# Turning the last channel-major products of a hybrid decoder layer into token-major ones

## The chip, the cores and the metric

One core of a Trainium2 chip runs the whole layer in one program. The time is the device time of one execution in microseconds, and the figure for a kernel is the median of its runs. Everything is float32 in and out.

## The reference

One layer for 256 tokens (T) with 2048 channels (D), and 256 memory tokens. A normalised x, `h`, goes through one wide product, whose columns are cut among three branches; each branch goes back to D through a product of its own, is scaled by a sigmoid gate, and the sum goes through an output product and a last norm.

```python
h = rms_norm(x, norm_w)
(sb_q, sb_k, sb_v, sb_z, ssd_z, ssd_xbc, ssd_dt, mem_q, mem_z, gate_pre) = split(h @ w_in)
o_sb  = stick_breaking_attention(sb_q, sb_k, sb_v) * silu(sb_z)           # 8 heads of 128
xbc   = silu(causal_depthwise_conv(ssd_xbc, conv_w, conv_b))              # 4 taps, 4096 channels
x_ssm, b_in, c_in = split(xbc)                                            # 2048, 1024, 1024
y     = ssd_chunked_scan(x_ssm, dt, a, b_in, c_in) + d_skip * x_ssm
o_ssd = gated_group_rms_norm(y, ssd_z, ssd_norm_w)                        # 8 groups of 256
o_mem = memory_cross_attention(mem_q, mem_n, w_mem_kv) * silu(mem_z)      # 4 heads of 256
g_sb, g_ssd, g_mem = split(sigmoid(gate_pre + b_gate))
merged = g_sb*(o_sb @ w_branch_sb) + g_ssd*(o_ssd @ w_branch_ssd) + g_mem*(o_mem @ w_branch_mem)
return rms_norm(x + merged @ w_out, final_norm_w)
```

## The kernel before

Nearly all of the time goes into products of 256 tokens with weights that stream in from DRAM, 0.5 MB at a time. Such a piece is a **chunk**. Its load `raw` goes out on SP's queue (`load_chunk`, L205; four buffers). The products are taken in halves: each value is split in two (`split`, L142): ACT copies it into the high half `wh` (L146, type fp32r), DVE subtracts that from the value for the low half `wl` (L150); three buffers of each. A product of float32 is then three products of halves: high by high, high by low, low by high.

There are two ways to take a product.

- **Token-major** (`gemm`, L249): the activations are stationary, 512 columns of the weights move. A chunk is 2 k-tiles of 128 rows by 512 columns. For each k-tile and each half of the tokens there are three matmuls of 512 columns (L266, L267, L268): 12 for a chunk. Out come rows of tokens, 512 channels wide. The accumulator is evacuated 3 chunks after the product's end (LATE).
- **Channel-major** (`gemm_cols`, L211): the weights are stationary, 128 by 128. What moves are the activations: both halves side by side, 512 wide, past `wh` (L229), and the high half alone, 256 wide, past `wl` (L233). A chunk is 4 k-tiles by 256 columns, so 16 matmuls. Out come channels on partitions, tokens along the row, in two accumulators that `fold` (L239) adds: an ACT copy (L246) and a DVE add (L247), 2 chunks after the end (LATE_C).

Steps that need channels on partitions are the attention heads (q and k), the convolution, whose taps run along the tokens, and the gates z. The z products are token-major already and are **turned** by `to_turned` (L298): DVE transposes blocks of 32 by 32 out of the accumulator (L307, twice), ACT's queue sends them to a scratch in DRAM (L309, twice), and four DMAs from ACT's queue bring them back with the blocks in order (L316). The result has its tokens in a permuted order; the views `turned` and `blocked` (L321, L326) read it.

Each engine runs its instructions in the order in which the program emits them. Beside the chunks, two mechanisms set that order. `defer(fn, n)` puts a step into a heap, to be emitted n chunks later. `pump` (L185), called after each chunk, emits what is due and then moves one of two lanes on by a step; the lanes hold the attention heads and the 8 SSD groups as generators. A step that comes to ACT or DVE stands between the splits of two chunks, and the splits behind it wait for it.

The order of the products, with their chunks: memory values (16), kT (16, channel-major), qM (16, channel-major), zM and zS (32, turned), qS and kS (32, channel-major), vS (16), zT (32, turned), the convolution's xBC (64, channel-major), then for each branch four pairs of a gate product (8 chunks) and a branch product (4, 4 or 8 chunks), then the output product. The memory heads run beside qS to zT, the stick-breaking heads beside zT and the convolution, the SSD groups beside the first and the second branch.

In the convolution, `conv_evac` (L708) folds 256 channels into a tile `cu` and defers the four taps of each 128 channels (L717, L720: one DVE instruction of 256 tokens and three of 255, 254, 253), so that the last are emitted 5 chunks after the product's end. A list `waiting` (L725) holds the 12 tiles that get a silu: four of z, then B, C, and the four of x. Three are emitted for each of the last four groups of 512 channels, the last three of x 1, 2 and 6 chunks behind the convolution's end. They share a table with the copies; ACT loads another for the exponentials (L741) and for the sigmoids (L745).

A gate product's evacuation (L880) adds the bias on DVE and defers `sigmoid` (L744) by one chunk; the branch product's evacuation (L889) multiplies with it. Inside `ssd_group` (L750), ACT copies `cbs` (L775), takes exponentials of `dec` (L785), DVE weighs them (L789), and the sums y are added into the x tiles of cT (L812, L815).

## Time and profile before

| what | before |
|---|---|
| median of 3 runs | 1226.38 us (1225.35 to 1226.67) |
| profiled execution | 1225.48 us, span of the trace 1223.7 us |
| granted clock of TensorE | 0.998 of full speed |
| TensorE matmuls (PE) | 1213.0 us busy, 99% |
| weight loads of TensorE (PEld) | 1024.1 us, 84% |
| VectorE (DVE) | 781.5 us, 64% |
| ScalarE (ACT) | 640.7 us, 52% |
| GpSimd (POOL) | 50.4 us, 4% |
| DMA | 251.07 MB, 205 GB/s on average |
| chain of waits that ended last | PE 96%, DMA 1%, ACT 1%, DVE 1%, issue 1% |
| largest group on DVE | L150, 409 x 1232 ns |
| largest group on ACT | L146, 409 x 1056 ns |

The profile is of one execution, and times in it count from the start of its span. "Busy" counts instructions from start to end; matmuls overlap one another, so their lengths add up to more than the time that they take, and the distance of their starts is the better measure. In a row of the timeline stand the start, the length (of several, where the row ends in x2), the engine, the line, the operation, the tiles written and read, and in brackets how long the engine was idle just before, and who ended that wait. A row of groups has the count, the busy time and the mean of one in ns behind the bar. A table load of ACT (ACT_TABLE_LOAD) takes 1283 ns.

### The profile page before, as it was taken

Reading aid. Unit: us, or ns where it says so; the run is one execution under the profiler, and the core shown is the slowest. Engines: PE = TensorE matmul, PEld = TensorE weight load, DVE = VectorE, ACT = ScalarE, POOL = GpSimd, SP = SyncE. Lnnn points to the kernel's source line nnn. Section 1 sums busy time; section 2 is a strip of 40 time slices with the busy share of each in tenths; the row PEclk is TensorE's granted clock in tenths of the full one; section 3 lists DMA queues with packets and bytes.
Section 4 is the critical chain, followed back from the end, with each engine's and each line's share of the span. In section 5 each row is a group of like instructions: output and inputs, shape, how many; then the busy total and the mean of one; then the engine's idle time right before and its main releaser. Section 6 shows DMA issues by size and latency. Waiting matters only on the chain.

```text
span 1223.7 us, 16119 instructions
## 1 busy us (share of the span) xinstructions
PE 1213.0 (99%) x6132; PEld 1024.1 (84%) x6132; DVE 781.5 (64%) x990; ACT 640.7 (52%) x859; POOL 50.4 (4%) x50
## 2 busy tenths in 40 slices
PE   9999999999999999999999999999999999999997
PEld 7888888888888888888888888888888888888886
DVE  5686564556654555888887758676677755555554
ACT  6764533364444444545665757475756544444443
POOL 0000000000000000010100000000000010110101
PEclk9999999999999999999999999999999999999999
DMA  9966578875466778655668667576856666567673
GB/s 308 364 201 191 156 233 230 244 204 155 149 179 189 223 217 232 183 176 177 177 184 221 208 198 222 180 232 180 233 182 189 204 194 210 185 196 243 201 245 112
DMA packets 169646, 251.07 MB, mean 205 GB/s; under 512 B 11040, under 2 KB 85984, under 8 KB 169440
## 3 DMA queue, kind: packets, MB, share of 16 engines
q1 hardware_dynamic: 151840, 229.51, 61.7%
q10 hardware_dynamic: 17728, 20.53, 5.6%
q8 instruction: 48, 0.79, 0.3%
q14 instruction: 30, 0.25, 0.1%
HBM read 243.68 MB, written 6.32 MB: 204 GB/s over the span
## 4 chain that ended last, share of the span: by engine, by line
PE 96%; DMA 1%; issue 1%; ACT 1%; DVE 1%; SPq 0%; POOLq 0%; POOL 0%; ACTq 0%
PE acc L266 20%; PE acc L267 19%; PE acc L268 19%; PE acc L229 19%; PE acc L233 10%; PE acc L429 1%; PE acc L430 1%; PE acc L428 1%; PE y L806 1%; DMA raw<-in_w_out_dram 1%; DMA raw<-in_w_mem_kv_dram 1%; DVE wl L150 0%; PE dtp L490 0%; PE mt L872 0%; PE xp L763 0%
## 5 line engine op out<-in xcount | busy, mean ns | idle before, releaser
L150 DVE TENSOR_TENSOR wl<-raw,wh 128x1024 fp32r<-128x1024 f32 (+1 forms) x409 | 502.8, 1232 | 327.1 <-ACT wh L146 325.1
L146 ACT ACTIVATE wh<-raw 128x1024 fp32r<-128x1024 f32 (+1 forms) x409 | 431.4, 1056 | 417.8 <-PE acc L268 277.6
L229 PE MATMUL acc<-hT,wh 128*128 128x512 f32 x896 | 282.5, 397 | 0.1
L266 PE MATMUL acc<-wh,hT 128*128 128x512 f32 x704 | 276.6, 393 | 0.0
L267 PE MATMUL acc<-wl,hT 128*128 128x512 f32 x704 | 274.3, 390 | 0.0
L268 PE MATMUL acc<-wh,hT 128*128 128x512 f32 x704 | 274.3, 390 | 0.0
L233 PEld LDWEIGHTS acc<-hT,wl 128*128 128x128 f32 x896 | 168.2, 188 | 40.7 <-DVE wl L150 1.0
L233 PE MATMUL acc<-hT,wl 128*128 128x256 f32 x896 | 176.2, 278 | 0.5 <-DVE wl L150 0.5
L268 PEld LDWEIGHTS acc<-wh,hT 128*128 128x128 f32 x704 | 132.2, 188 | 27.9
L266 PEld LDWEIGHTS acc<-wh,hT 128*128 128x128 f32 x704 | 132.2, 188 | 27.3 <-ACT sq L146 0.5
L267 PEld LDWEIGHTS acc<-wl,hT 128*128 128x128 f32 x704 | 132.3, 188 | 26.8 <-DVE wl L150 0.6
L229 PEld LDWEIGHTS acc<-hT,wh 128*128 128x128 f32 x896 | 136.6, 189 | 0.5 <-ACT wh L146 0.3
L266 PE MATMUL acc<-wh,oD 128*128 128x512 f32 x128 | 49.8, 389 | 0.0
L267 PE MATMUL acc<-wl,oD 128*128 128x512 f32 x128 | 49.8, 389 | 0.0
L268 PE MATMUL acc<-wh,oD 128*128 128x512 f32 x128 | 49.8, 389 | 0.0
L720 DVE SCALAR_TENSOR_TENSOR cT<-cu,wcols,cT 128x255 f32<-128x255 f32 (+2 forms) x96 | 46.4, 483 | 3.4
L892 POOL TENSOR_TENSOR merged<-merged,sig 128x512 f32<-128x512 f32 x16 | 25.1, 1590 | 521.5 <-DVE sig L891 521.5
L229 PE MATMUL acc<-memT,wh 128*128 128x512 f32 x128 | 40.5, 398 | 0.0
L266 PE MATMUL acc<-wh,mT 128*128 128x512 f32 x96 | 37.4, 390 | 0.0
L268 PE MATMUL acc<-wh,mT 128*128 128x512 f32 x96 | 37.4, 389 | 0.0
L267 PE MATMUL acc<-wl,mT 128*128 128x512 f32 x96 | 37.4, 389 | 0.0
L233 PEld LDWEIGHTS acc<-memT,wl 128*128 128x128 f32 x128 | 24.0, 188 | 5.9 <-DVE wl L150 0.3
(245 smaller groups left out, 1280.3 us busy)
## 6 DMA issues: line engine op xcount, KB each, us to landing
raw<-in_w_in_dram SPq DMA_DIRECT2D x288, 512.0 KB, 4.2
raw<-in_w_branch_ssd_dram SPq DMA_DIRECT2D x32, 512.0 KB, 4.3
raw<-in_w_out_dram SPq DMA_DIRECT2D x32, 512.0 KB, 4.9
raw<-in_w_mem_kv_dram SPq DMA_DIRECT2D x31, 512.0 KB, 6.2
raw<-in_w_branch_mem_dram SPq DMA_DIRECT2D x16, 512.0 KB, 3.8
raw<-in_w_branch_sb_dram SPq DMA_DIRECT2D x16, 512.0 KB, 4.8
dec<-acT SPq DMA_DIRECT2D x24, 256.0 KB, 6.4
turned<-blocks ACTq DMA_DIRECT2D x16, 256.0 KB, 4.4
```

Source lines behind the costliest of these rows:

```text
L146: nc.scalar.activation(hi, src, AF.Copy, **({} if scale is None else {"scale": scale}))
L150: nc.vector.tensor_tensor(lo, src, h32, ALU.subtract)
L229: nc.tensor.matmul(halves[b], wh[:, kt - k0, b * P:(b + 1) * P], lhs.both(kt), start=first, stop=False, skip_group_check=True)
L233: nc.tensor.matmul(halves[b][:, 1], wl[:, kt - k0, b * P:(b + 1) * P], lhs.at(kt)[0], start=False, stop=last, skip_group_check=True)
L266: nc.tensor.matmul(a, lh[:, tt], wh[:, j], start=first, stop=False)
L267: nc.tensor.matmul(a, lh[:, tt], wl[:, j], start=False, stop=False)
L268: nc.tensor.matmul(a, ll[:, tt], wh[:, j], start=False, stop=last)
L428: nc.tensor.matmul(a, lh[:, tt], wh[:, g], start=first, stop=False)
L429: nc.tensor.matmul(a, lh[:, tt], wl[:, g], start=False, stop=False)
L430: nc.tensor.matmul(a, ll[:, tt], wh[:, g], start=False, stop=last)
L720: nc.vector.scalar_tensor_tensor(a[:, s:T], u[:, 0:T - s], convw[:, 3 - s, i:i + 1], a[:, s:T], ALU.mult, ALU.add)
L892: nc.gpsimd.tensor_tensor(merged[t][:, cs], merged[t][:, cs], sig[:, t], ALU.add)
```

## The change

All channel-major products (kT, qM, qS, kS and the convolution's xBC, 128 chunks) become token-major products of 512 columns by `gemm`, which takes `ready` and `acc` from its callers for that. `to_turned` is built on a new helper, `turning`: both block transposes go into one tile `blocks` (one buffer) when the accumulator is evacuated; one DMA takes them out one chunk later; four DMAs bring them back two chunks behind that, either into the result itself, as for z, or into a tile `turned` (one buffer), which a function `use` reads three chunks later. For kT and qM `use` is two splits, for qS and kS one ACT copy, and for the convolution two ACT copies into `cu` tiles, from which the taps of the four blocks are deferred by 1, 3, 5 and 7 chunks. From the end of a convolution product to its last taps it is now 3 + 1 + 2 + 3 + 7 = 16 chunks.

The list of silus is emitted as before, but for the last two x groups: only one is emitted with the last group, and the two that stay in the list are done by `silu_late`, one at the head of each of the first two sigmoids. The assertion in `wait_x`, which says how much of the normalised x must have been emitted ahead, is loosened by one step. The small tiles `cbs` get buffers of their own in place of sharing `cu`'s.

```diff
-    def gemm(lhs, nk, w, c0, evac):
+    def gemm(lhs, nk, w, c0, evac, ready=None, acc=None):
...
-    def to_turned(dst, g):
+    def turning(use=None, dst=None):
+
+        scratch = dram.tile([2, P, 4, 4, 32], F32, name=nm("scratch"))
+
+        def evac(rows):
+            blocks = tmp.tile([P, 2, 4, 4, 32], F32, tag="blocks", name=nm("blocks"), bufs=1)
             for t in range(2):
+                nc.vector.transpose(blocks[:, t].rearrange("p j k c -> p k j c"),
+                                    rows[t].rearrange("p (k j c) -> p k j c", k=4, j=4))
+            defer(lambda: away(blocks), 1)
+
+        def away(blocks):
+            nc.scalar.dma_start(scratch.rearrange("t p j k c -> p t (j k c)"),
+                                blocks.rearrange("p t j k c -> p t (j k c)"))
+            defer(back, 2)
 
         def back():
+            cols = dst
+            if dst is None:
+                cols = tmp.tile([P, 8, P], F32, tag="turned", name=nm("turned"), bufs=1)
             for j in range(4):
                 nc.scalar.dma_start(
                     cols[32 * j:32 * j + 32],
                     scratch[:, :, j].rearrange("t (i r) k c -> r (t i) (k c)", r=32))
+            if use is not None:
+                defer(lambda: use(cols), 3)
         return evac
...
+    def tiles(cols, k, n):
+        return cols.rearrange("p i (k c) -> p k i c", c=32)[:, k:k + n]
+
+    def split_turned(dst, g):
+        def use(cols):
+            for k in (0, 2):
+                split((*[blocked(a) for a in dst.at(4 * g + k, 2)], tiles(cols, k, 2), None))
+        return turning(use)
+
+    def copy_turned(dst, g):
+        return turning(lambda cols: nc.scalar.activation(
+            blocked(dst[:, 4 * g:4 * g + 4]), tiles(cols, 0, 4), AF.Copy))
...
-    def conv_evac(i0):
-        def evac(acc):
-            u = tmp.tile([P, 2, T], F32, tag="cu", name=nm("cu"), bufs=2)
-            fold(u, acc)
-            for b in range(2):
-                defer(lambda b=b: taps(u[:, b], i0 + b), 1 + 2 * b)
+    def conv(i0):
+        def use(cols):
+            for k in (0, 2):
+                u = tmp.tile([P, 2, T], F32, tag="cu", name=nm("cu"), bufs=2)
+                nc.scalar.activation(blocked(u), tiles(cols, k, 2), AF.Copy)
+                for b in range(2):
+                    defer(lambda u=u, i=k + b: taps(u[:, i % 2], i0 + i), 1 + 2 * (k + b))
...
     for i, g in enumerate((4, 5, 6, 7, 0, 1, 2, 3)):
-        for j in range(2):
-            gemm_cols(hT, NKT, w_in, C_XBC + g * GW + 2 * j * P, conv_evac(4 * g + 2 * j))
+        gemm(hT, NKT, w_in, C_XBC + g * GW, conv(4 * g))
         waiting.append(cT[g // 2][:, 4 * (g % 2):4 * (g % 2) + 4])
         if i >= 4:
-            for j in range(3):
-                silu(waiting.pop(0), 6 if not waiting else 1 + j)
+            for j in range(3 if i < 7 else 1):
+                silu(waiting.pop(0), 1 + j)
+
+    def silu_late():
+
+        if waiting:
+            g = 4 - len(waiting)
+            assert all(4 * g + i in tapped for i in range(4)), (g, tapped)
+            a = waiting.pop(0)
+            nc.scalar.activation(a, a, AF.Silu)
...
     def sigmoid(a):
+        silu_late()
         nc.scalar.activation(a, a, AF.Sigmoid)
         tables[0] = False
```

Three places of the order, first on ACT around the first sigmoid, from the last chunk of the first gate's branch product (the split ahead of it) to the second chunk of the second gate product. `wh` are the splits of chunks, `sig` is the gate, `dec` belongs to an SSD group, `cT` is an x tile. Before:

```order
L146 ACTIVATE wh_6057<-raw_6055 128x1024
L745 ACT_TABLE_LOAD
L745 ACTIVATE sig_5773<-sig_5773 128x1024
L877 DMA sig_6076<-in_b_gate_dram 128x512
L146 ACTIVATE wh_6081<-raw_6079 128x1024
L741 ACT_TABLE_LOAD
L785 ACTIVATE dec_5940<-dec_5940,nac 128x128 x2
L785 ACTIVATE dec_5942<-dec_5942,nac 128x128 x4
L146 ACTIVATE wh_6107<-raw_6105 128x1024
```

And of the changed kernel:

```order
L146 ACTIVATE wh_5605<-raw_5603 128x1024
L769 ACT_TABLE_LOAD
L769 ACTIVATE cT_3780<-cT_3780 128x1024
L783 ACT_TABLE_LOAD
L783 ACTIVATE sig_5301<-sig_5301 128x1024
L915 DMA sig_5629<-in_b_gate_dram 128x512
L146 ACTIVATE wh_5634<-raw_5632 128x1024
L778 ACT_TABLE_LOAD
L823 ACTIVATE dec_5476<-dec_5476,nac 128x128 x2
L823 ACTIVATE dec_5478<-dec_5478,nac 128x128 x4
L146 ACTIVATE wh_5660<-raw_5658 128x1024
```

Between two splits of chunks there stand now a table load and a silu more, ahead of the sigmoid with its own table load. Three chunks ahead of this the convolution's last two copies into `cu` have come between two splits, beside the copy of `cbs` that stood there alone.

Second, DVE at the same place, from the split of the second chunk of the second gate product on. `merged` is the first branch product's evacuation, `y` the sums of an SSD group. Before:

```order
L150 TENSOR_TENSOR wl_6108<-raw_6105,wh_6107 128x1024
L150 TENSOR_TENSOR wl_6139<-raw_6136,wh_6138 128x1024
L889 TENSOR_TENSOR merged_5771<-acc_5979,sig_5773 128x512
L889 TENSOR_TENSOR merged_5772<-acc_5979,sig_5773 128x512
L789 TENSOR_TENSOR dec_5940<-dec_5940,cbs_6000 128x512
L789 TENSOR_TENSOR dec_5942<-dec_5942,cbs_6000 128x512
L150 TENSOR_TENSOR wl_6161<-raw_6158,wh_6160 128x1024
```

And of the changed kernel:

```order
L150 TENSOR_TENSOR wl_5661<-raw_5658,wh_5660 128x1024
L745 TENSOR_SCALAR cT_3780<-cu_5540,wcols 128x256
L748 SCALAR_TENSOR_TENSOR cT_3780<-cu_5540,wcols,cT_3780 128x255
L748 SCALAR_TENSOR_TENSOR cT_3780<-cu_5540,wcols,cT_3780 128x254
L748 SCALAR_TENSOR_TENSOR cT_3780<-cu_5540,wcols,cT_3780 128x253
L150 TENSOR_TENSOR wl_5696<-raw_5693,wh_5695 128x1024
L927 TENSOR_TENSOR merged_5299<-acc_5519,sig_5301 128x512
L927 TENSOR_TENSOR merged_5300<-acc_5519,sig_5301 128x512
L827 TENSOR_TENSOR dec_5476<-dec_5476,cbs_5544 128x512
L827 TENSOR_TENSOR dec_5478<-dec_5478,cbs_5544 128x512
L150 TENSOR_TENSOR wl_5718<-raw_5715,wh_5717 128x1024
```

A set of taps of the convolution's last group has come between two splits, and another such set follows behind the last row, where before the convolution's taps were all emitted ahead of this place.

Third, ACT around the second sigmoid, at the end of the second branch product. `xs` belongs to the first SSD group's norm. Before:

```order
L146 ACTIVATE wh_6339<-raw_6337 128x1024
L745 ACT_TABLE_LOAD
L745 ACTIVATE sig_6076<-sig_6076 128x1024
L741 ACT_TABLE_LOAD
L831 ACTIVATE xs_5916<-tot_6311,eps 128x256
L832 ACTIVATE xs_5916<-xs_5916 128x256
```

And of the changed kernel:

```order
L146 ACTIVATE wh_5900<-raw_5898 128x1024
L769 ACT_TABLE_LOAD
L769 ACTIVATE cT_3780<-cT_3780 128x1024
L783 ACT_TABLE_LOAD
L783 ACTIVATE sig_5629<-sig_5629 128x1024
L778 ACT_TABLE_LOAD
L869 ACTIVATE xs_5452<-tot_5872,eps 128x256
L870 ACTIVATE xs_5452<-xs_5452 128x256
```

Here, too, a table load and a silu have come ahead of the sigmoid's. The table loads of the whole program go from 23 to 25.

More of the change, by code (lines that the diff above doesn't have):

```diff
@@ L84, in small2 @@
     def small2(shape, n):
-        return tmp.tile(shape, F32, tag="cu", name=nm(n), bufs=2)
+        return tmp.tile(shape, F32, tag="cbs", name=nm(n), bufs=2)
     def bank(shape, n="bank"):
@@ L247, in fold @@
             nc.vector.tensor_tensor(dst, acc[:, :, 0], dst, ALU.add)
-    def gemm(lhs, nk, w, c0, evac):
-        acc2 = psA.tile([P, 2, GW], F32, tag="acc", name=nm("acc"), bufs=2)
-        acc = [acc2[:, 0], acc2[:, 1]]
+    def gemm(lhs, nk, w, c0, evac, ready=None, acc=None):
+        if acc is None:
+            acc2 = psA.tile([P, 2, GW], F32, tag="acc", name=nm("acc"), bufs=2)
+            acc = [acc2[:, 0], acc2[:, 1]]
         kc = KC
         for k0 in range(0, nk, kc):
+            if ready is not None:
+                ready(k0)
             raw = load_chunk(w, c0, GW, k0, kc)
@@ L295, in to_rows @@
         return evac
-    def to_turned(dst, g):
-        scratch = dram.tile([2, P, 4, 4, 32], F32, name=nm("turned"))
-        cols = dst[:, 4 * g:4 * g + 4].rearrange("p k t -> p (k t)").rearrange(
-            "p (i n) -> p i n", n=P)
-        def evac(acc):
-            for t in range(2):
-                blocks = ta([P, 4, 4, 32], "blocks")
-                nc.vector.transpose(blocks.rearrange("p j k c -> p k j c"),
-                                    acc[t].rearrange("p (k j c) -> p k j c", k=4, j=4))
-                defer(lambda t=t, blocks=blocks: nc.scalar.dma_start(
-                    scratch[t].rearrange("p j k c -> p (j k c)"),
-                    blocks.rearrange("p j k c -> p (j k c)")), 1)
-            defer(back, 3)
+    def turning(use=None, dst=None):
+        scratch = dram.tile([2, P, 4, 4, 32], F32, name=nm("scratch"))
+        def evac(rows):
+            blocks = tmp.tile([P, 2, 4, 4, 32], F32, tag="blocks", name=nm("blocks"), bufs=1)
+            for t in range(2):
+                nc.vector.transpose(blocks[:, t].rearrange("p j k c -> p k j c"),
[5 more added lines that the diff above has]
+            defer(back, 2)
         def back():
+            cols = dst
+            if dst is None:
+                cols = tmp.tile([P, 8, P], F32, tag="turned", name=nm("turned"), bufs=1)
             for j in range(4):
@@ L469, in trunk_kernel @@
     kT = Cols(8, "kT")
-    for g in range(4):
-        gemm_cols(memT, NKT, w_mem_kv, 2 * g * P, to_split_cols(kT, 2 * g),
-                  acc=None if g else [bank([P, 2, T], "acc") for _ in range(2)])
+    for g in range(2):
+        gemm(memT, NKT, w_mem_kv, g * GW, split_turned(kT, g),
+             acc=None if g else [bank([P, GW], "acc") for _ in range(2)])
     finish()
@@ L557, in trunk_kernel @@
     zS = slot([P, 8, T], F32, "zS")
-    for g in range(4):
-        gemm_cols(hT, NKT, w_in, C_MEMQ + 2 * g * P, to_split_cols(qM, 2 * g),
-                  ready=None if g else wait_x)
+    for g in range(2):
+        gemm(hT, NKT, w_in, C_MEMQ + g * GW, split_turned(qM, g),
+             ready=None if g else wait_x)
     for dst, c0 in ((zM, C_MEMZ), (zS, C_SBZ)):
@@ L631, in trunk_kernel @@
     for dst, c0 in ((qS, C_SBQ), (kS, C_SBK)):
-        for g in range(4):
-            gemm_cols(hT, NKT, w_in, c0 + 2 * g * P, to_cols(dst, 2 * g))
+        for g in range(2):
+            gemm(hT, NKT, w_in, c0 + g * GW, copy_turned(dst, g))
     for g in range(2):
@@ L722, in taps @@
                                                ALU.mult, ALU.add)
-        return evac
+            tapped.add(i)
+        return turning(use)
+    tapped = set()
     waiting = [zT[i // 2][:, 4 * (i % 2):4 * (i % 2) + 4] for i in range(4)]
     for i, g in enumerate((4, 5, 6, 7, 0, 1, 2, 3)):
-        for j in range(2):
-            gemm_cols(hT, NKT, w_in, C_XBC + g * GW + 2 * j * P, conv_evac(4 * g + 2 * j))
+        gemm(hT, NKT, w_in, C_XBC + g * GW, conv(4 * g))
         waiting.append(cT[g // 2][:, 4 * (g % 2):4 * (g % 2) + 4])
         if i >= 4:
-            for j in range(3):
-                silu(waiting.pop(0), 6 if not waiting else 1 + j)
+            for j in range(3 if i < 7 else 1):
[6 more added lines that the diff above has]
+            nc.scalar.activation(a, a, AF.Silu)
     oD = []
```

10 lines of the change are left out of this document (7 added, 3 removed).

## The prediction

> **What bounds the kernel now.** I read the page first: TensorE (PE) is busy for the whole span, and DVE and ACT, which cut each weight chunk into its two halves, are far from full. Then I read who PE waited for.
>
> ```profile
> PE 1213.0 (99%) x6132; PEld 1024.1 (84%) x6132; DVE 781.5 (64%) x990; ACT 640.7 (52%) x859; POOL 50.4 (4%) x50
> PE acc L233 <- DVE wl L150: 0.5, 1, 0.5
> ```
>
> The second row is the longest wait of PE behind a split, 0.5 us. So the time is what PE needs for its matmuls, plus whatever stall a change makes. The question is how fast the two kinds of product stream. The timeline of PE shows both: two rows of a channel-major product eight k-tiles apart, and two rows of a token-major one seven triples apart (start, length, instruction).
>
> ```profile
> 249.72 0.63 PE L229 MATMUL acc<-hT,wh 128*128 128x512 f32 x2
> 255.29 0.63 PE L229 MATMUL acc<-hT,wh 128*128 128x512 f32 x2
> 180.90 0.39 PE L268 MATMUL acc<-wh,hT 128*128 128x512 f32 x1
> 185.66 0.39 PE L268 MATMUL acc<-wh,hT 128*128 128x512 f32 x1
> ```
>
> Channel-major: 5.57 us for 8 k-tiles of 256 columns, 0.696 us each (two matmuls of 512, two of 256). Token-major: 4.76 us for 7 triples of 512, 0.680 us for the same 128 x 256 piece of weight. The starts count here, not the lengths, which overlap.
>
> **PE's own work.** The page has L229 1024 times (896 with hT, 128 with memT), two for each k-tile: 512 k-tiles of 256 columns. 512 x (0.696 - 0.680) = 8.3 us less. Nothing on PE is added. The Trainium skill, "TensorE: Matmul & The Clock Gate", section "Back-to-back issue gap", gives N / 2.4 + 2.5 ns, by which the four short and long matmuls would cost only 2.5 ns more than three long ones, 1.3 us in all. The rows above show 16 ns, and I take them.
>
> **The evacuations.** For 512 columns before: two folds, each an ACT copy and a DVE add. Now: two block transposes on DVE, five DMA issues on ACT, and two copies or splits on ACT. The rows of the groups (count, total, mean ns), those of tile cu, those of tile turned (ns min/median/max), and the page's row of the way out (KB, us to landing):
>
> ```profile
> L307 DVE STREAM_TRANSPOSE blocks<-acc 128x512 f32<-128x512 f32 x16 | 10.4, 690 | 0.0
> L246 ACT ACTIVATE cu<-acc x16: 597/598/600, 487.3 to 663.4; 128x512 f32<-128x512 f32 x16
> L247 DVE TENSOR_TENSOR cu<-acc,cu x16: 681/691/692, 487.9 to 664.1; 128x512 f32<-128x512 f32 x16
> L316 ACTq DMA_DIRECT2D zT<-turned x16: 325/467/536, 414.0 to 486.0; - x16
> turned<-blocks ACTq DMA_DIRECT2D x16, 256.0 KB, 4.4
> DMA to landing us min/median/max: 3.6/5.5/7.2
> ```
>
> DVE does not change: 2 x 690 against 2 x 691 ns. ACT keeps its two copies of 0.6 us and gains 4 x 0.47 + 0.35 = 2.2 us of issues for each of 16 new turnings, 35 us over the kernel on an engine that is half idle. PE hides it as long as ACT's queue is not late by more than about 3.2 us: a chunk is four triples on PE, 2.72 us; there are three buffers of wh, so a wh is free to be written two chunks (5.4 us) ahead of its use, and its split takes some 1.0 on ACT and 1.2 on DVE. The way back waits on ACT for the way out's landing (4.4 us; the way back stands two chunks, 5.4 us, behind it) and the copy for the way back's (three chunks, 8.2 us, less 1.8 of issues, against the 5.5 to 7.2 of the last row). That is close, but it fits. The eight turnings of today have the first of these waits and cost PE nothing. I take 0.4 us in all for the places where it meets a silu or the second half of an attention head in the convolution, between 0 and 3.
>
> **A stall that goes.** At 322.85 ACT stood for 3.4 us before a fold of kS, waiting for PE. A softmax step and a wh were queued behind it, and PE ran dry for 1.1 us in sum around 331:
>
> ```profile
> 322.85 0.60 ACT L246 ACTIVATE kS<-acc 128x512 f32<-128x512 f32 x1 [3.40 <-PE acc L233]
> 331.23 0.73 PE L229 MATMUL acc<-hT,wh 128*128 128x512 f32 x2
> 332.49 0.50 PE L233 MATMUL acc<-hT,wl 128*128 128x256 f32 x2 [0.53 <-DVE wl L150]
> ```
>
> From 331.23 to 332.49 are 1.26 us where 0.46 is usual, and some 0.3 lie before and behind. Now four DMA issues stand there in place of the fold. Late next is the same softmax step, so I book -0.8, not -1.1.
>
> **The first late silu.** Two silus of the x groups move from behind the convolution into the first two sigmoids, where each brings a table load of its own. Around the first, ACT has no gap after 684.74, and PE gets its split with little to spare (ACT, DVE, PE):
>
> ```profile
> 684.74 0.49 ACT L775 ACTIVATE cbs<-cb 128x384 f32<-128x384 f32 x1 [0.67 <-PE cb L768]
> 690.54 1.05 ACT L146 ACTIVATE wh<-raw 128x1024 fp32r<-128x1024 f32 x1
> 691.61 1.28 ACT L745 ACT_TABLE_LOAD   x1
> 692.90 1.06 ACT L745 ACTIVATE sig<-sig 128x1024 f32<-128x1024 f32 x1
> 693.87 1.04 ACT L146 ACTIVATE wh<-raw 128x1024 fp32r<-128x1024 f32 x1
> 697.99 1.99 ACT L146 ACTIVATE wh<-raw 128x1024 fp32r<-128x1024 f32 x2
> ...
> 699.07 2.36 DVE L150 TENSOR_TENSOR wl<-raw,wh 128x1024 fp32r<-128x1024 f32 x2 [2.30 <-ACT wh L146]
> 701.35 1.28 DVE L889 TENSOR_TENSOR merged<-acc,sig 128x512 f32<-128x512 f32 x2
> 702.55 1.28 DVE L789 TENSOR_TENSOR dec<-dec,cbs 128x512 f32<-128x512 f32 x2
> 703.75 1.22 DVE L150 TENSOR_TENSOR wl<-raw,wh 128x1024 fp32r<-128x1024 f32 x1
> 705.28 0.87 DVE L812 SCALAR_TENSOR_TENSOR cT<-cT,wcols,y 128x256 f32<-128x256 f32 x2 [0.32 <-PE y L806]
> 706.19 0.69 DVE L815 TENSOR_TENSOR zT<-zT,cT 128x512 f32<-128x512 f32 x1
> ...
> 701.12 0.39 PE L267 MATMUL acc<-wl,hT 128*128 128x512 f32 x1
> 705.16 0.50 PE L266 MATMUL acc<-wh,hT 128*128 128x512 f32 x1
> ```
>
> The wh at 697.99 belongs to the second chunk of the second gate product. Its wl is done near 700.25, and PE asks for it at 701.12: 0.87 us to spare. Table and sigmoid take 693.87 - 691.61 = 2.26, and a table with a silu as much. Two copies of the convolution, 1.2 by the row of tile cu, stand ahead as well; 0.67 of them falls into the gap at 684.74, 0.5 remains. So that wl comes 2.76 later: a stall of about 1.8.
>
> Behind it the taps of the last group, which used to be done by 675, now stand between DVE's splits. One set is 0.41 + 3 x 0.48 = 1.86 us by these rows:
>
> ```profile
> L717 DVE TENSOR_SCALAR cT<-cu,wcols x32: 404/407/1115, 490.4 to 672.6; 128x256 f32<-128x256 f32 x32
> L720 DVE SCALAR_TENSOR_TENSOR cT<-cu,wcols,cT x96: 481/483/486, 490.8 to 674.1; 128x255 f32<-128x255 f32 x32, 128x254 f32<-128x254 f32 x32, 128x253 f32<-128x253 f32 x32
> ```
>
> From that wl to the end of the wl three chunks on, DVE then has taps 1.86, wl 1.14 (2.36 less 1.22), merged 1.2, decay 1.2, wl 1.14, taps 1.86, y 0.87, z 0.65, wl 1.14: 11.1 us. PE covers the same stretch in 705.16 - 701.12 + 2 x 2.72 + 0.35 = 9.8. Another 1.3.
>
> Ahead of it the DMAs are full, and ACT's burst began when a late raw arrived:
>
> ```profile
> 660.00:680.00 20.00, 20.00 (x97) 16.77 (x96) 14.78 (x23) 10.24 (x12) 0.00 (x0) 1.00 0.97 256
> 678.88 1.06 ACT L146 ACTIVATE wh<-raw 128x1024 fp32r<-128x1024 f32 x1 [1.90 <-DMA raw<-in_w_in_dram]
> ```
>
> The first row is the window of 660 to 680, DMA share 0.97. The last turning now puts 0.5 MB out and 0.5 MB back into it. At 256 GB/s that is up to 4 us, and whatever of it that raw bears starts the burst later and is lost whole: 0 to 3.1, I take 0.9. The first site costs 1.8 + 1.3 + 0.9 = 4.0, between 1 (if copies and taps fall in gaps) and 6.2.
>
> **The second late silu.** At the second sigmoid PE had nothing to spare already:
>
> ```profile
> 727.39 1.28 ACT L745 ACT_TABLE_LOAD   x1
> 728.68 1.06 ACT L745 ACTIVATE sig<-sig 128x1024 f32<-128x1024 f32 x1
> 729.76 1.28 ACT L741 ACT_TABLE_LOAD   x1
> 732.54 2.00 ACT L146 ACTIVATE wh<-raw 128x1024 fp32r<-128x1024 f32 x2
> ...
> 733.63 2.36 DVE L150 TENSOR_TENSOR wl<-raw,wh 128x1024 fp32r<-128x1024 f32 x2 [4.93 <-ACT wh L146]
> ...
> 734.53 0.39 PE L266 MATMUL acc<-wh,hT 128*128 128x512 f32 x1
> 734.90 0.50 PE L267 MATMUL acc<-wl,hT 128*128 128x512 f32 x1
> ```
>
> PE's L267 follows its L266 by 0.37 instead of 0.23, because wl was only then done. Table and silu put 729.76 - 727.39 = 2.4 us ahead of that wh, with nothing to take it up: 2.4, between 1.8 and 2.8. What the silus leave behind the convolution frees ACT where it does not bind: nothing.
>
> **The sum.** -8.3 - 0.8 + 0.4 + 4.0 + 2.4 = -2.3 us. The profiled execution took 1225.48 us (span 1223.7) and would take 1223.2; the median of the runs is 0.9 above it, so 1226.38 becomes 1224.1. Within 0.2%, about 2.45 us, no difference can be told by a measurement of this kernel.
>
> **Rivals.** (1) The cover holds better: that raw is not late, and the taps fall into DVE's gaps. Then the first site costs 1.8 and the rest stands: -8.3 - 0.8 + 0.4 + 1.8 + 2.4 = -4.5, 1221.9. For it speaks that DVE sat idle 2.3 us just there (699.07); against it, that the DMAs are at 0.97. (2) The turnings block ACT, and the kernel becomes slower: the way back lands late among the weights, the copy at the head of ACT's queue waits, and every wh behind it. It decides from a landing of some 9 us on: 6.3 us are covered, 2.7 then wait, and with a copy's 1.0 that is over the 3.2 of slack by 0.5. At 16 new turnings it is 8 us in place of the 0.4, 1231.7. For it speaks the 7.2 at the top of today's landings; against it, that no turning of today stalls PE. (3) The short matmuls are not what the k-tile pays for, as the skill's rule would have it. Then -1.3 stands in place of -8.3: 1231.1. The rows speak against it, since both cadences are of long undisturbed stretches of the same run.
>
> **Chances.** The forecast 0.56, with a range of its own from 1221.9 to 1226.5: 0.23 of it faster by over 0.2%, 0.33 within. Rival 1 0.22, rival 2 0.18, rival 3 0.04. So faster 0.45, same 0.33, slower 0.22. The range runs from 1220.0, where the first site costs next to nothing, to 1230.0, where the dear ends of both sites and of the convolution (6.2 + 2.8 + 3) meet and part of rival 2 lies.
>
> **What would show it.** Starts of L267 to L267 0.680 us a triple in all products of before's L229. Gaps of PE before L267 of the second and fifth chunk of the second gate product, 4 us together, and one of 2.4 us at the third gate product's first chunk, all released by wl. No gap of over 0.5 us in the convolution, or else rival 2. If those three gaps are missing, the gain is near 9 us and my ACT queue was wrong; if PE's k-tile stays at 0.696, the cadence was.

## The result, and the profile after

The changed kernel takes 1232.38 us (median of 6 runs, 1230.13 to 1235.82), beside 1225.68 us for the kernel before (6 runs). The ratio is 1.0055, with a 95% interval of 1.0038 to 1.0072: 6.7 us slower, where the prediction had 2.3 us faster and ended its range at 1230. Its runs also lie further apart (5.7 us, before 1.3).

The profiled execution took 1234.59 us, its span 1232.8. That is 2.2 us above the median: the two profiled executions lie 9.1 us apart, the medians 6.7. The page gives the engines, the chain of waits and the DMAs of the turnings (KB, median us to landing):

```profile
PE 1211.3 (98%) x5620; PEld 1000.3 (81%) x5620; DVE 779.7 (63%) x989; ACT 640.2 (52%) x848; POOL 47.9 (4%) x50
...
PE 84%; DMA 7%; ACT 4%; DVE 3%; issue 2%; ACTq 0%; SPq 0%; POOLq 0%; POOL 0%; DVEq 0%
...
scratch<-blocks ACTq DMA_DIRECT2D x24, 512.0 KB, 4.2
turned<-scratch ACTq DMA_DIRECT2D x64, 128.0 KB, 6.1
```

DVE and ACT have no more work than before. But the chain, which was PE for 96%, now runs through DMA, ACT and DVE for 14%. The waits of PE say behind whom (total, times, longest):

```profile
PE acc L270 <- DVE wl L150: 5.9, 8, 1.1
PE acc L269 <- ACT wh L146: 3.6, 3, 2.0
```

What was to be gained did come. Two rows of the changed convolution, seven triples apart, are 4.76 us from start to start, 0.680 each:

```profile
561.51 0.39 PE L271 MATMUL acc<-wh,hT 128*128 128x512 f32 x1
...
566.27 0.39 PE L271 MATMUL acc<-wh,hT 128*128 128x512 f32 x1
```

To see where it went, I cut the timeline of PE at the first matmul of each product, and took the lengths. Below, each kernel's difference to the profile of before, in us; g0, g1, g2 are the first gate products, m0 and m1 the branch products between them. The names are those of the experiments further down.

```
                    values+kT   qM    qS    kS   conv    g0    m0    g1    m1    g2
changed                +1.4   -0.9  -1.0  -2.0   -2.9  +6.5   0.0  +3.0  +1.5  +2.5
x1_tail_cols           -0.8   -0.9  -1.0  -2.0   -0.6  +0.8   0.0   0.0   0.0   0.0
x2_no_late_silu        +1.9   -0.9  -1.0  -2.0   -1.9  +1.6   0.0  +2.0   0.0   0.0
x3_conv_cols           +0.1   -0.9  -1.0  -2.0    0.0   0.0   0.0   0.0   0.0   0.0
x4_back_later          +0.4   -0.9  -1.0  -2.0   -2.4  +1.3  +1.6  +3.8  +1.5  +2.5
y1_late_silu_alone     -0.2   -0.8  -1.0  -2.0   -0.2  +0.8   0.0  +1.7  +1.5  +2.4
y2_filled_stall        -1.7   -0.9  -1.0  -2.0   -1.6  +4.3   0.0  +3.7  +1.7  +1.2
y3_first_half          +1.6   -0.9  -1.0  -2.0   +3.3   0.0   0.0   0.0   0.0   0.0
z1_silu_at_3_and_5     -1.0   -0.9  -1.0  -2.0   -1.7  +5.2   0.0  +0.6   0.0   0.0
z2_back_later_too      +1.5   -0.9  -1.0  -2.0   -1.9   0.0   0.0  +1.7   0.0   0.0
z4_ssd_later           -1.2   -0.7  -1.0  -2.0   -2.4  +2.2  +4.2  +1.7  +1.5  -1.1
```

The changed kernel loses 13.4 us between g0 and g2. Everything from behind g2 to the output product is the same to 0.1 us in all of them but the last, which loses 10 more there. (The last stretch, from the first matmul of the last 512 output columns to the end, took 30.7 to 32.4 us in these executions, with the same code; 1.1 of the 9.1 us lie there.)

The changed kernel and all kernels below also ask for `dynamic_dma_scratch_size=1024` where the program is built, which the diff of the change leaves out. In the products that the change does not touch (zM and zS, vS, zT) their lengths agree with those of before to 0.05 us, so no effect of it is seen.

**The first gate product, +6.5.** ACT's timeline (ACTq are issues of DMAs from its queue) shows it standing before the last turning's way back:

```profile
666.23 0.42 ACTq L313 DMA_DIRECT2D scratch<-blocks  x1
666.77 2.20 ACT L146 ACTIVATE wh<-raw 128x1024 fp32r<-128x1024 f32 x2 [4.18 <-DVE blocks L308]
674.60 2.97 ACTq L322 DMA_DIRECT2D turned<-scratch  x4
677.62 0.49 ACT L813 ACTIVATE cbs<-cb 128x384 f32<-128x384 f32 x1 [8.64 <-DMA turned<-scratch]
678.00 2.00 ACT L146 ACTIVATE wh<-raw 128x1024 fp32r<-128x1024 f32 x2
```

The way out is issued at 666.23, and the first way back at 674.60: 8.4 us for the landing, not 4.4. From 669.0 on the way back stands at the head of ACT's queue; ACT stands for 5.6 us and then issues for 3 more, with the split of a chunk behind it. PE ran dry:

```profile
679.11 0.49 PE L269 MATMUL acc<-wh,hT 128*128 128x512 f32 x1 [1.98 <-ACT wh L146]
680.37 0.50 PE L270 MATMUL acc<-wl,hT 128*128 128x512 f32 x1 [0.77 <-DVE wl L150]
...
681.63 0.63 PE L271 MATMUL acc<-wh,hT 128*128 128x512 f32 x1
682.05 0.63 PE L269 MATMUL acc<-wh,hT 128*128 128x512 f32 x1
```

Start to start against the usual 0.227, it lost 2.1 us before the L269 and 1.0 before the L270: once the wh is late, PE waits for DVE's half of the same chunk as well. And behind the stall two starts are 0.427 us apart. The windows show why (PEclk is the third number from the end):

```profile
680.60:681.10 0.50, 0.50 (x3) 0.41 (x3) 0.50 (x1) 0.50 (x1) 0.00 (x0) 1.00 0.28 66
681.10:684.51 3.41, 3.41 (x9) 2.59 (x9) 2.47 (x6) 3.40 (x9) 0.00 (x0) 0.50 0.55 150
684.51:686.00 1.49, 1.49 (x11) 1.33 (x10) 1.49 (x3) 0.80 (x3) 0.00 (x0) 1.00 0.93 362
```

The granted clock is 0.50 for 3.41 us behind the stall: 8 matmuls by 0.2 us, another 1.6.

That is not yet all of the 6.5. The first three chunks of g0 had lost 1.6 us before, behind the turning ahead of the last. ACT stood for 4.0 us until its way back had landed; the two copies and the silu of an x group came behind that, then the split that PE waited for (ACT, DVE, PE):

```profile
657.65 1.16 ACT L739 ACTIVATE cu<-turned 128x512 f32<-128x512 f32 x2 [3.97 <-DMA turned<-scratch]
658.71 1.04 ACT L203 ACTIVATE cT<-cT 128x1024 f32<-128x1024 f32 x1
...
660.73 1.22 DVE L150 TENSOR_TENSOR wl<-raw,wh 128x1024 fp32r<-128x1024 f32 x1 [4.46 <-ACT wh L146]
...
662.01 0.50 PE L270 MATMUL acc<-wl,hT 128*128 128x512 f32 x1 [0.76 <-DVE wl L150]
```

**The second late silu, +1.5 and +2.5.** Here the change does what was foreseen, and a little more:

```profile
731.48 1.28 ACT L769 ACT_TABLE_LOAD   x1
732.77 1.06 ACT L769 ACTIVATE cT<-cT 128x1024 f32<-128x1024 f32 x1
733.85 1.28 ACT L783 ACT_TABLE_LOAD   x1
...
739.01 2.95 ACT L146 ACTIVATE wh<-raw 128x1024 fp32r<-128x1024 f32 x3
...
740.11 0.50 PE L269 MATMUL acc<-wh,hT 128*128 128x512 f32 x1 [1.33 <-ACT wh L146]
741.37 0.50 PE L270 MATMUL acc<-wl,hT 128*128 128x512 f32 x1 [0.76 <-DVE wl L150]
```

The table and silu take 733.85 - 731.48 = 2.37 us, and PE loses 1.5 + 1.0 = 2.5, counted from start to start. The window behind it shows the half clock again:

```profile
742.54:745.95 3.41, 3.41 (x11) 2.73 (x10) 3.34 (x6) 0.04 (x1) 0.00 (x0) 0.50 1.05 255
```

Six matmuls by 0.2 us are 1.2 more. Together it is nearly all of the 4.0 of m1 and g2 in the table.

### The profile page after: what moved, and what is told of

It is laid out like the page before. It is cut to its first block, busy times and chain, and to the rows that moved or that the text cites. A ratio compares the mean times of both kernels' runs of the same rounds, so it can differ in the third digit from the quotient of the medians.

```text
span 1232.8 us, 15176 instructions
## 1 busy us (share of the span) xinstructions
PE 1211.3 (98%) x5620; PEld 1000.3 (81%) x5620; DVE 779.7 (63%) x989; ACT 640.2 (52%) x848; POOL 47.9 (4%) x50
## 4 chain that ended last, share of the span: by engine, by line
PE 84%; DMA 7%; ACT 4%; DVE 3%; issue 2%; ACTq 0%; SPq 0%; POOLq 0%; POOL 0%; DVEq 0%
PE acc L270 26%; PE acc L269 26%; PE acc L271 26%; DMA turned<-scratch 2%; DVE wl L150 2%; DMA scratch<-blocks 1%; ACT wh L146 1%; DMA raw<-in_w_out_dram 1%; PE y L844 1%; DMA rows<-in_x_dram 1%; DMA rows<-in_mem_dram 1%; DMA raw<-in_w_mem_kv_dram 1%; DVE cT L748 0%; PE acc L456 0%; PE acc L457 0%
## 5 line engine op out<-in xcount | busy, mean ns | idle before, releaser
L269 PE MATMUL acc<-wh,hT 128*128 128x512 f32 x1152 | 454.0, 394 | 3.4 <-ACT wh L146 3.3
L270 PE MATMUL acc<-wl,hT 128*128 128x512 f32 x1152 | 451.0, 392 | 4.2 <-DVE wl L150 4.1
L271 PE MATMUL acc<-wh,hT 128*128 128x512 f32 x1152 | 450.0, 391 | 0.0
L270 PEld LDWEIGHTS acc<-wl,hT 128*128 128x128 f32 x1152 | 217.2, 188 | 51.0 <-DVE wl L150 8.1
L269 PEld LDWEIGHTS acc<-wh,hT 128*128 128x128 f32 x1152 | 216.9, 188 | 49.2 <-ACT wh L146 5.1
L271 PEld LDWEIGHTS acc<-wh,hT 128*128 128x128 f32 x1152 | 217.0, 188 | 45.5
L269 PE MATMUL acc<-wh,oD 128*128 128x512 f32 x128 | 49.8, 389 | 0.0
L270 PE MATMUL acc<-wl,oD 128*128 128x512 f32 x128 | 49.8, 389 | 0.0
L269 PE MATMUL acc<-wh,mT 128*128 128x512 f32 x96 | 37.4, 390 | 0.0
L270 PE MATMUL acc<-wl,mT 128*128 128x512 f32 x96 | 37.4, 389 | 0.0
L308 DVE STREAM_TRANSPOSE blocks<-acc 128x512 f32<-128x512 f32 x48 | 31.4, 692 | 0.0
L271 PEld LDWEIGHTS acc<-wh,oD 128*128 128x128 f32 x128 | 24.0, 188 | 5.0
L270 PEld LDWEIGHTS acc<-wl,oD 128*128 128x128 f32 x128 | 24.0, 188 | 5.0
L269 PEld LDWEIGHTS acc<-wh,oD 128*128 128x128 f32 x128 | 24.0, 188 | 4.9
L270 PE MATMUL acc<-wl,memT 128*128 128x512 f32 x64 | 25.1, 393 | 1.8 <-DVE wl L150 1.8
L455 PE MATMUL acc<-wh,memT 128*128 128x512 f32 x64 | 25.1, 393 | 1.5 <-ACT memT L146 1.5
```

The lines of the kernel that those rows point to most:

```text
L269: nc.tensor.matmul(a, lh[:, tt], wh[:, j], start=first, stop=False)
L270: nc.tensor.matmul(a, lh[:, tt], wl[:, j], start=False, stop=False)
L271: nc.tensor.matmul(a, ll[:, tt], wh[:, j], start=False, stop=last)
L308: nc.vector.transpose(blocks[:, t].rearrange("p j k c -> p k j c"), rows[t].rearrange("p (k j c) -> p k j c", k=4, j=4))
L455: nc.tensor.matmul(a, lh[:, tt], wh[:, g], start=first, stop=False)
```

## The experiments

Theory A, formed on these rows: the turnings are hidden nearly everywhere, and the loss is one way back at the head of ACT's queue, where the way out lands late, and the two late silus at places without slack. The rivals were that the turnings cost by their DMAs everywhere (B), that the weights themselves are late at the convolution's end (C), and that the silus only suffer from a queue that is late already (D). All kernels are the changed one with the edit shown.

### x1_tail_cols: two groups channel-major again, silus as before

```diff
+        if i < 6:
             gemm(hT, NKT, w_in, C_XBC + g * GW, conv(4 * g))
+        else:
+            for j in range(2):
+                gemm_cols(hT, NKT, w_in, C_XBC + g * GW + 2 * j * P, conv_evac(4 * g + 2 * j))
...
-            for j in range(3 if i < 7 else 1):
-                silu(waiting.pop(0), 1 + j)
+            for j in range(3):
+                silu(waiting.pop(0), 6 if not waiting else 1 + j)
```

> The changed kernel, but the last two groups of the convolution stay channel-major with folds, and all silus stand behind the convolution as before. Theory A (the loss is one late way back of the last turning, at the head of ACT's queue, and the two late silus; the turnings elsewhere are hidden): 448 of the 512 k-tiles gain 16 ns each, -7.2, and the kS fold's stall -0.8, nothing against it: 1225.7 - 8.0 = 1217.7 us, up to 1220 if the stall of 1.8 us in kT returns. Rival B (the 16 new turnings cost by their DMAs all over the kernel, as the 2.3 us that the convolution lost of its gain would have it): half of the gain is eaten everywhere, 1221 to 1224 us.

1221.51 us (5 runs, 1220.81 to 1222.92), ratio 0.9963 (0.9951 to 0.9975). The number is B's, the place is not: every four chunks of the convolution gain 0.24 us up to its last quarter, and all of the loss lies in its last 8 chunks, 2.3 us, and in g0. So the loss belongs to a place, as A has it, but A had not seen this place.

### x2_no_late_silu

```diff
-            a = waiting.pop(0)
-            nc.scalar.activation(a, a, AF.Silu)
+            waiting.pop(0)
```

> The changed kernel without the two late silus; two x tiles go on without their silu, so that part of the computation is left out, and two table loads with it. Theory A: the second sigmoid's loss (1.5 in the second branch product and 2.5 in the third gate product) is all the silu's, -4.0; the first site loses its table and silu, about -2 of the 3.0 in the second gate product, and keeps its taps; the 6.5 us in the first gate product stay. 1232.4 - 6 = 1226.4 us. Rival B (DMAs and taps, not the silus): no more than the 4.8 us of ACT's own work at most half on the path, 1230 us.

1225.31 us (12 runs, 1222.13 to 1228.26). The two silus are worth 7.1 us; m1 and g2 are as before. A holds. g1 keeps 2.0 of its loss, which A puts down to the late taps.

### x3_conv_cols: only kT, qM, qS and kS token-major

```diff
-        gemm(hT, NKT, w_in, C_XBC + g * GW, conv(4 * g))
+        for j in range(2):
+            gemm_cols(hT, NKT, w_in, C_XBC + g * GW + 2 * j * P, conv_evac(4 * g + 2 * j))
```

(and the silus as in x1_tail_cols)

> Only kT, qM, qS and kS token-major; the whole convolution and its silus as before. Theory A: 256 k-tiles by 16 ns, -4.1, and -0.8 for the kS fold: 1225.7 - 4.9 = 1220.8 us. If the stall of 1.8 us that the changed kernel's kT shows belongs to the change and is not of that one execution: 1222.6 to 1223 us. Rival B (turnings cost by their DMAs everywhere): 1224 or more.

1221.71 us (5 runs, 1220.85 to 1222.57), ratio 0.9961 (0.9949 to 0.9974). qM, qS and kS give what was reckoned, kT does not. It beats both kernels without touching the convolution.

### x4_back_later: the last way back four chunks behind

```diff
-            defer(back, 2)
+            defer(back, gap)
...
-        return turning(use)
+        return turning(use, gap=4 if i0 == 12 else 2)
```

> The changed kernel; the last turning alone brings its blocks back four chunks behind the way out instead of two, and its copies and taps come two chunks later. Theory A: the landing of 8.3 us is then covered by four chunks (10.9 us), ACT does not stand for 5.6 us, PE does not wait, and the clock stays up: 4 to 5 of the 6.5 us in the first gate product go, 1227.5 to 1228.5 us. Rival C (the weights themselves are late there, since the DMAs are full, and ACT would have waited anyway): 1231 us or more, and ACT's wait is then named after a raw.

1230.41 us (5 runs, 1229.63 to 1231.37). Half of what A expected. g0 loses 1.3 instead of 6.5, all of it in its first three chunks, ahead of the last turning. The runs lie 1.7 us apart instead of 5.7. But copies and taps now come at the first sigmoid, and m0 and g1 lose 2.4 more. The stall moved.

### y1_late_silu_alone

As x1_tail_cols, without its second hunk: the silus stay late.

> The kernel with the last two convolution groups channel-major (1221.5 us) and the two last silus at the sigmoids, as the changed kernel has them. So the late silus stand alone, without the last turning and its late taps. Theory A (the late silus have a price of their own, which is that of ACT's instructions and of the half clock behind the stall): the first site hides most (0 to 1.0), the second costs 1.5 in the second branch product and 2.5 in the third gate product: 1221.5 + 4 to 5 = 1225.5 to 1226.5 us. Rival D (the silus only hurt because DVE and ACT are late from the turning and the taps): under 1 us in all, 1221.5 to 1222.5.

1226.83 us (11 runs, 1224.94 to 1230.34): 5.3 us above x1_tail_cols, for the late silus alone, a little more than A had. m1 and g2 lose 1.5 and 2.4, as in the changed kernel, the half clock among them, and the first site hides less than I thought (g1 loses 1.7). Rival D falls.

### y2_filled_stall

```diff
+                    for n in range(fill[0] if first and t == 0 else 0):
+                        nc.tensor.matmul(acc[1][:, 0:P], ones, ones, start=True, stop=True)
                     nc.tensor.matmul(a, lh[:, tt], wh[:, j], start=first, stop=False)
+                    for n in range(fill[1] if first and t == 0 else 0):
+                        nc.tensor.matmul(acc[1][:, 0:P], ones, ones, start=True, stop=True)
...
+                 fill=(8, 6) if (br, g) == (0, 2) else (0, 0))
```

> The changed kernel; in the third gate product's first chunk PE does 8 small matmuls of ones before its first matmul and 6 behind it, into the half of the accumulator that is started anew later, while it waits for the split. Theory (the clock halves because PE stood idle for 2.5 of some 3 us): the granted clock stays at 1.00, no matmul there takes 0.427 us, and the third gate product takes 1.2 us less, 25.8 instead of 27.0 us. Rival (the half clock has another cause, the power or the DMAs): 27.0 or a little more, and 0.5 in the same place.

One run, 1228.48 us. The windows over the same place:

```profile
735.00:738.00 3.00, 3.00 (x27) 2.92 (x26) 1.42 (x2) 3.00 (x5) 0.00 (x0) 1.00 0.29 87
738.00:741.00 3.00, 3.00 (x18) 2.55 (x17) 2.93 (x5) 0.44 (x1) 0.00 (x0) 1.00 0.68 216
```

The clock stays at 1.00, and g2 takes 25.74 us instead of 27.04, with 0.2 more in m1. That is what the theory expected of idleness as the cause. In the three other profiles with this stall (the changed kernel, x4, y1) the clock halved. But y2 is one execution, and in the same one PE waited 2.0 + 1.0 us in g0, unfilled, and its clock stayed up there too; so chance is not ruled out. The run's distance to the others is no measure of it.

### y3_first_half and y4_kT_cols

```diff
+        if i < 4:
             gemm(hT, NKT, w_in, C_XBC + g * GW, conv(4 * g))
+        else:
+            for j in range(2):
+                gemm_cols(hT, NKT, w_in, C_XBC + g * GW + 2 * j * P, conv_evac(4 * g + 2 * j))
```

(silus as in x1_tail_cols; y4 also takes the changed lines of kT back)

> Token-major as changed, but of the convolution only the first four groups (B and C, beside which no silu stands); the x groups channel-major and all silus as before. Theory A (a turning is hidden where ACT has no silus, and costs where silus, late taps and full DMAs meet): the 1221.7 us with the whole convolution channel-major, less 32 chunks by 0.0625, 2.0 us: 1219.7 us. Rival B (turnings cost by their DMAs everywhere): 1221.5 us or more, as with six groups.

> As the kernel with the first four convolution groups token-major, and kT channel-major again. Theory A (kT gains nothing token-major: behind the memory values ACT and DVE are the bound, and what PE saves it waits): within 0.5 us of that kernel, some 1219.7 us. Rival E (kT's turnings cost there, as the 1.8 us of the changed kernel's profile would say): 1 to 2 us less, 1218. Rival F (kT gains its 1.0 like qM): 1220.7 us.

y3 took 1225.14 us (11 runs, 1224.03 to 1227.71), y4 1224.55 (11 runs, 1223.71 to 1226.50). The first misses A's 1219.7 by 5.4 us. The loss lies at the seam, in 12 chunks (200 to 211 of the program), which take 5.2 us more than before. There the taps of the last token-major group, up to 16 chunks late, meet the folds and taps of the first channel-major ones. DVE, then ACT:

```profile
613.57 0.41 DVE L745 TENSOR_SCALAR cT<-cu,wcols 128x256 f32<-128x256 f32 x1
614.02 1.52 DVE L748 SCALAR_TENSOR_TENSOR cT<-cu,wcols,cT 128x255 f32<-128x255 f32 x3
615.46 1.22 DVE L150 TENSOR_TENSOR wl<-raw,wh 128x1024 fp32r<-128x1024 f32 x1
616.59 0.41 DVE L763 TENSOR_SCALAR cT<-cu,wcols 128x256 f32<-128x256 f32 x1
617.04 1.52 DVE L766 SCALAR_TENSOR_TENSOR cT<-cu,wcols,cT 128x255 f32<-128x255 f32 x3
618.47 0.42 DVE L713 TENSOR_TENSOR so<-spo,zS 128x256 f32<-128x256 f32 x1
...
618.92 0.42 ACT L146 ACTIVATE oS<-so 128x256 fp32r<-128x256 f32 x1 [6.01 <-DVE so L713]
```

Two sets of taps (L745 and L763 are the two kinds) to one split fill DVE; a step of a head waits behind them, and ACT stands for 6 us before it. Read so, it is a price of late taps, and of DMAs none: in that stretch (590 to 650) neither ACT nor PE waits for a DMA. No run moved these taps alone. Between y3 and y4 lie 0.6 us: on the whole, kT gains nothing by being token-major.

### z1_silu_at_3_and_5

```diff
+        sigmoids[0] += 1
-        if waiting:
+        if sigmoids[0] in (3, 5):
```

> The changed kernel, with the two late silus at the third and the fifth sigmoid instead of the first and the second. The trace of before shows there 2.8 us and more to spare between a wl and its matmul for ten chunks, against 0.8 and 0.05 us behind the first and the second; a table and a silu take 2.4. The SSD groups that read these x tiles start later still. Theory A (the price of a late silu is what the slack at its place leaves): nothing is left of it, 1225.3 us, as without these silus. Rival D (the two tables and silus cost wherever they stand): 1229 to 1232 us.

1225.37 us (11 runs, 1221.75 to 1227.04): 7.0 us less than the changed kernel, and the same as without these silus. The work is all there, at another place. ACT, DVE and PE at the third sigmoid:

```profile
762.11 1.28 ACT L772 ACT_TABLE_LOAD   x1
763.40 1.06 ACT L772 ACTIVATE cT<-cT 128x1024 f32<-128x1024 f32 x1
764.48 1.28 ACT L786 ACT_TABLE_LOAD   x1
...
767.82 1.23 DVE L150 TENSOR_TENSOR wl<-raw,wh 128x1024 fp32r<-128x1024 f32 x1 [4.13 <-ACT wh L146]
...
770.88 0.40 PE L270 MATMUL acc<-wl,hT 128*128 128x512 f32 x1
```

The wl is done at 769.05, and its L270 starts at 770.88 without a wait. The slack was there to be had.

### z2_back_later_too

z1_silu_at_3_and_5 with the edit of x4_back_later, and one line:

```diff
-                silu(waiting.pop(0), 1 + j)
+                silu(waiting.pop(0), 1 + j if i < 7 else 4)
```

> As the kernel with the late silus at the third and fifth sigmoid, and the last turning's way back four chunks behind its way out instead of two; the silu of the second x group, which waited for taps, comes three chunks later. Theory A (what is left is ACT standing before the way back and before taps): 1 to 2 us less than that kernel, 1223.5 to 1224.5 us, with runs closer together. Rival C (the weights are late there, not ACT): the same as that kernel.

1221.65 us (7 runs, 1220.15 to 1224.40), ratio 0.9968 (0.9956 to 0.9979): 3.7 us less than z1, more than expected. The runs are hardly closer together (4.3 us apart, z1's 5.3), which was expected too. Now ACT goes on splitting while the way out lands, and the first gate product takes what it took before:

```profile
671.69 1.05 ACT L146 ACTIVATE wh<-raw 128x1024 fp32r<-128x1024 f32 x1
674.75 1.06 ACT L146 ACTIVATE wh<-raw 128x1024 fp32r<-128x1024 f32 x1 [2.00 <-DVE wl L150]
674.78 1.85 ACTq L322 DMA_DIRECT2D turned<-scratch  x4
```

Rival C falls: the weights were not late. The 1.6 us of g0's first chunks are gone as well; the copy there stood for 1.9 us instead of 4.0, and a silu came later, and which of the two did it is not shown. x4_back_later had gained little because the same steps met the silu at the first sigmoid.

### z3_q_and_k_alone

x3_conv_cols with kT channel-major as well.

> Only qM, qS and kS token-major; kT and the convolution channel-major, all silus as before. Theory A (qM and qS gain 1.0 each, kS 2.0, kT nothing): 1225.8 - 4.0 = 1221.8 us, the same as with kT token-major (1221.7), within 0.6 us. Rival E (kT's turnings cost 1 or more): 1220.7 us or less. Rival F (kT gains like qM): 1222.7 us.

1221.64 us (5 runs, 1220.57 to 1222.75), ratio 0.9966 (0.9955 to 0.9978). A's 1221.8.

### z4_ssd_later

```diff
-    defer(start_ssd, 4)
+    defer(start_ssd, 8)
```

(on top of z1_silu_at_3_and_5)

> As the kernel with the late silus at the third and fifth sigmoid, and the SSD groups start eight chunks behind the convolution instead of four, so that their six loads of 256 KB come behind the last turning. Theory A (the last way out lands late because these loads fill the DMAs, and ACT stands behind it): the stall in the first gate product goes (1.6 to 6.5 us in the profiles so far), the taps of the last group no longer meet the decays: 1222 to 1224 us, and runs closer together. Rival C (the turning's landing is late from the weights alone): no change from that kernel, 1225 us, or worse, as the SSD groups end four chunks later.

1236.10 us (4 runs, 1235.68 to 1237.38): the other way, by 11 us. The profile parts this in two. SP's issues of the SSD groups' loads (dec), and ACT:

```profile
665.54 1.58 SPq L800 DMA_DIRECT2D dec<-acT  x3
...
678.21 2.93 SPq L800 DMA_DIRECT2D dec<-acT  x3
...
663.98 0.38 ACTq L313 DMA_DIRECT2D scratch<-blocks  x1
669.34 3.78 ACTq L322 DMA_DIRECT2D turned<-scratch  x4
682.26 1.15 ACT L739 ACTIVATE cu<-turned 128x512 f32<-128x512 f32 x2 [4.09 <-DMA turned<-scratch]
```

The loads did not come behind the turning, as was expected: three went out 1.6 us behind the way out, three after the way back. In the changed kernel three had gone 12 us ahead of the way out, and three just with it (665.46 beside 666.23). Now the way back was issued 5.4 us behind the way out, where four executions with the loads earlier had 7.4 to 8.4. That speaks for the loads as what made the landing late, in one execution. But now they meet the way back, and the copy stood for 4.1 us in its turn. The rest of the loss, m0 to the end of the SSD groups, comes where the groups' steps fall on other chunks of the gate products, with 6.8 us of half clock in the fourth; I did not take it apart further.

### w1_back_later_x and w2_taps_later

```diff
-        return turning(use, gap=4 if i0 == 12 else 2)
+        return turning(use, gap=4 if i0 in (4, 8, 12) else 2)
...
-                    defer(lambda u=u, i=k + b: taps(u[:, i % 2], i0 + i), 1 + 2 * (k + b))
+                    defer(lambda u=u, i=k + b: taps(u[:, i % 2], i0 + i),
+                          1 + 2 * (k + b) if i0 < 12 or i0 > 15 else 15 + 2 * (k + b))
```

(on top of z2_back_later_too; the second hunk in w2 alone)

> As the kernel with the last way back later (1221.65 us), with the ways back of the last three convolution groups, instead of the last alone, four chunks behind their ways out. In its profile the turning before the last made ACT stand for 3.7 us until 649.5, and PE lost 1.1 us at 652.5. Theory A: that stall goes, 1 us less, 1220.6 us. Rival (the convolution loses to late taps and silus, not to ways back): no change, 1221.7 us.

> As that, and the taps of the last group come 15, 17, 19 and 21 chunks behind its copies instead of 1, 3, 5 and 7, in the third gate product, where before had 2.6 us and more to spare; their silu stands at the fifth sigmoid, behind them. Theory A (1.7 us of the second gate product were taps between DVE's splits): 1.7 us less than the other kernel of this pair, 1219 us. Rival (the stall comes from DVE's sum of work and moves with the taps): no change, 1220.6 us.

w1 took 1222.83 us (11 runs, 1219.88 to 1224.70), w2 1221.13 (5 runs, 1219.24 to 1224.39; ratio 0.9959, 0.9945 to 0.9972). Neither is told apart from z2. In w1's profile the convolution gains 1.0 more than in z2's, and g0 and g1 lose 2.7 more. In w2's, the last four chunks of g1, which had lost 1.2 in z2 and w1, lose nothing, so that this loss was the taps'; but others lose instead. What the convolution's end still loses moves with every step that is moved.

## Why the prediction was wrong

**PE's own work, -8.3.** Right in the rate. qM and qS gave 0.9 and 1.0 each, kS 1.0 beside its stall, and the convolution 0.24 for each four chunks until its last quarter. The formula of the Trainium skill, "TensorE: Matmul & The Clock Gate", section "Back-to-back issue gap", does not fit that: by its N / 2.4 + 2.5 ns a k-tile would have given 2.5 ns, and the runs show 15. The same section says that the formula is for an isolated matmul and comes out too low for short ones and too high for long ones; the prediction's third rival applied it to a stream, which it does not claim to describe. Too high for long ones is not borne out here: 227 ns from start to start, where it gives 216.

Wrong in one part: kT gave nothing on the whole. Over 13 profiles with kT token-major, values and kT together differ from before by -1.7 to +1.9, 0.0 on average. The rate came there too: kT's last twelve chunks took 32.64 us in all 13, and 33.44 in the three profiles with kT channel-major, which is the 0.8 that belongs to them. But its first four took 12.0 to 14.8 us, 13.3 on average, against 12.0 to 12.6. I had let all 512 k-tiles count and put the seam behind the memory values at nothing. What makes that stall longer in some executions stays open.

**The stall of kS, -0.8.** Right: 2.0 less in kS, of which 1.0 is the rate.

**The evacuations, +0.4, and the late raw, 0.9.** This step failed. I read the way out's landing off a median (4.4 us), and set it against two chunks (5.4 us): "close, but it fits". I had quoted the DMA share of 0.97 at the convolution's end myself, but booked it to a raw, with 0.9 us. It was the last way out that bore it. The changed kernel's 24 ways out have about the same median, and another top:

```profile
DMA to landing us min/median/max: 3.7/4.2/8.3
```

The 8.3 is the last one; the other 23 landed within 5.8. In the eight profiles that have this turning beside the SSD groups' loads it took 7.3 to 10.0 us. Where the way back came two chunks behind (the changed kernel, x2, y2 and z1), ACT stood for 4.7 to 5.6 us; PE lost 1.2 to 3.2 of it, and 1.6 more where the clock halved (the changed kernel and z1). The cover of the turning ahead, 6.4 us for its way back, failed as well: the copy stood for 4.0 us in the changed kernel, and g0's first chunks lost 1.6. In all, g0 lost 1.6 to 6.5 us in these four. Part of the spread between the runs may come from this, since x4's runs lie within 1.7 us; but those of z2, w1 and w2, with the same later way back, lie 4.3 to 5.2 us apart, so the spread stays unexplained.

**The first late silu, 1.8 + 1.3.** Right: the silu alone cost 1.7 in g1 (y1), the taps without it 0.6 to 2.0 (z1 and x2), and both together 3.0 in the changed kernel, most of it at the two chunks that were named, the second and the fifth.

**The second late silu, 2.4.** The mechanism was right, the size was off: 4.0 in three kernels (the changed one, x4, y1). The stall itself was 2.5. The term that was missing is the half clock behind it, 1.2 us, which was gone in y2.

**Rival 2** came near in its time (1231.7) by chance, with the last two turnings in place of sixteen. It took the way back's landing for the one that decides, and priced each turning at half a microsecond. The convolution's first quarters show that price to be nothing, and by the prediction's own sign, a gap of over 0.5 us in the convolution, the rival is out: PE's one wait there in the changed kernel is of 0.2 us. What made the kernel slower was the end of the last two turnings, in g0, and 5 us or more from the silus: 5.3 by y1, 7.1 by x2. By place, x2's profile gains 5.0 us on the changed kernel's in g1, m1 and g2. It gains as much again in g0, which lies ahead of the first late silu and where its instructions are the same, so that some of the 7.1 may be chance.

What stays open is why the convolution's last quarter loses 0.6 to 2.4 us. Copies, silus, taps and the last heads all stand there, and moving one (w1, w2) moved the loss.

## What to carry to other kernels

A step that is off the critical path has a price that its place sets: the same two silus cost 5 to 7 us at the first two sigmoids and nothing that the runs can tell at the third and fifth. Before moving a step, list for each chunk how early its split is done, and put the step where that margin is larger than the step. And take a DMA's landing, if an in-order engine will stand before it, from the stage where it lands, not from the median of the kernel.

## What the hardware showed

Two waits of PE, the first of 1.4 to 2.1 us and the second of 1.0, with one matmul between them, were followed by 3.41 us at a granted clock of 0.50 (the changed kernel twice; x4, y1 and z1 once each), and 2.3 + 1.0 in z4 by 6.83 us, twice that. It wasn't so every time: y2 had 2.0 + 1.0 in g0, x4 1.2 + 1.0 at the seam of m0 and g1, and both kept their clock. The Trainium skill ("TensorE: Matmul & The Clock Gate", section "Part 1: The HAM clock gate (the "warmup" mystery)") has a window of about 3.4 us that runs free of the program. The stretches of 3.41 and 6.83 us agree with its length. That only some stalls are punished would fit a window that runs free, but no run here shows the window itself. The Trainium skill's rule that no idle gap should be over 3.4 us (same page, section "HAM oscillation — how this bites in real kernels") is too mild here: 2.4 us in two pieces were enough in z1.

The waits of SP name another one that I had not looked for (total, times, longest): a load of weights waited on the landing of a way back.

```profile
SPq L207 <- DMA turned<-scratch: 10.2, 2, 9.4
```

PE did not feel it in this profile, since no raw was late behind it. I made no run of it.
